# Full-height products and one transpose for the delta net's last chunk

## The chip, the cores and the metric

The kernel runs on one core of a Trainium2 chip. The metric is device time in microseconds for one execution of the whole program; lower is better. The core has a matrix engine (TensorE, PE in the profile; PEld is its weight load), a vector engine (DVE), a scalar engine (ACT), GpSimd (POOL), and DMA queues that SyncE (SP) issues here.

## The reference, cut to what matters

One inference step of a two-layer decoder trunk over 304 tokens: 16 meta tokens, 256 prompt tokens, and 8 sequences of 4 new tokens. Every layer projects the normalised input once, runs four groups of mixers beside each other (gated delta net, RG-LRU, GLA, retention), gates their outputs and projects back. The change lies in the gated delta net, in its chunked form:

```python
a = jnp.where(strict, jnp.einsum('bihk,bjhk->bhij', kb, kc) * decay, 0.0)
sol = lax.linalg.triangular_solve(a + eye, rhs, left_side=True, lower=True)
u, w = sol[..., :dv], sol[..., dv:]
v_new = u - jnp.einsum('bhik,bhkv->bhiv', w, s)
attn = jnp.einsum('bihk,bjhk->bhij', qc, kc) * decay
o = (jnp.einsum('bihk,bhi,bhkv->bihv', qc, jnp.exp(gcum), s)
     + jnp.einsum('bhij,bhjv->bihv', attn, v_new))
s_new = (s * jnp.exp(g_last)[..., None, None]
         + jnp.einsum('bjhk,bhj,bhjv->bhkv', kc, jnp.exp(g_last[..., None] - gcum), v_new))
```

There are 4 delta heads a layer, with keys and values of width 128, and each sequence has a state of 128x128.

## The kernel before

**Layout.** Activations stand transposed: 128 features on the partitions, the 304 tokens along a row. The tokens make three chunks (`CH`): 0 to 127, 128 to 255, and a last one of 48, which holds the last 16 prompt tokens and the 32 new ones (`TP` = 272 is where the new ones begin). A product contracts over partitions, so work on the last chunk contracts over 48 tokens, or over the 16 prompt tokens alone.

**Main products.** A layer's input projection is 48 tiles of 128 columns, its output projection 16. A weight tile comes in four units of 4x128 rows; ACT splits a unit into `hi`, DVE into `lo`, and PE makes three products for each 128 rows (`main<-xh,hi`, `main<-xl,hi`, `main<-xh,lo`). That is 48 main matmuls a tile. On SP the weight loads (`raw`) share one queue with all small transfers.

**Everything else** runs as threads between the main matmuls. After each main product `Threads.poll` lets every thread whose inputs are ready advance by one step; whether they are ready is reckoned by `Clocks` from prices that `price` holds for each instruction. This program runs when the kernel is built, and the order it comes to is fixed: a changed price or a changed instruction can move any later step. `take` and `give` lend buffers by the same clocks. `deltas` runs `delta_thread` for heads 0 and 1, then for heads 2 and 3; it writes PSUM tiles named d. The other mixers write tiles named e. `gate_thread` takes the outputs `o` in the order of `GATES`, heads 2 and 3 last, and makes `m`, on which the output projection waits. ACT changes its function table (an ACT_TABLE_LOAD of line 359) when a step wants Silu after Exp or Ln, or the other way.

**The end of a delta pair, line by line.** `KN[h]` holds normalised keys, padded with zeros from column 304 to 383 (line 917). `VB[h]` holds scaled values by token; its last chunk is 48 rows. `uf[h][:, 2]` is the inverse of the last chunk's triangle; its columns 64 to 127 are a copy of the new tokens' columns. Lines 1109 to 1117 scale its 48 rows into `SL` and multiply them by a constant `st` (a 48-row product for each head). Lines 1122 and 1123 transpose the last chunk's keys: 64 columns of `KN`, and then `twice` makes two matmuls with the identity that put the 32 new tokens' keys on partitions 64 to 95 and 96 to 127. `hi_lo` reads these for the state update, and line 1126 has ACT copy the 16 prompt rows into `LQ`. Lines 1137 and 1138 make the new values `VN` of the chunk, the first of the two products over 48 rows; line 1145 updates the prompt state over 16 rows; line 1153 adds the chunk's attention over 48 rows to the output. Then `o_norm` normalises the output and `stash` hands it to the gates.

Of the kernel before, what the change touches and what calls it, by code (L numbers as in the profile page):

```python
# [12 lines left out]
AF = mybir.ActivationFunctionType  # L13
# [5 lines left out]
T = 304  # L19
TP = 272  # L20
# [323 lines left out]
def trunk(ctx: ExitStack, tc: tile.TileContext, I, O):  # L344
    nc = tc.nc
    clk = Clocks()
    pe, act, dve, pool, sp = (Engine(e, k, clk) for e, k in ((nc.tensor, "P"), (nc.scalar, "A"), (nc.vector, "V"),
                                                             (nc.gpsimd, "G"), (nc.sync, "S")))
# [7 lines left out]
    def tables(func):  # L356
        want = SETS.get(func)
        if want and table[0] not in want:
            nc.scalar.preload_act_table_set(want[0])  # L359
            clk.t["A"] += 1.3  # L360
            table[0] = want[0]

    def activ(out, in_, func, **kw):
        tables(func)
        act.activation(out, in_, func, **kw)
# [35 lines left out]
    def C(name, a=0, n=1):  # L401
        return cst[:, CC[name] + a:CC[name] + a + n]
# [5 lines left out]
    ident = C("id", 0, 128)  # L408
# [8 lines left out]
    col = one.tile([128, 4, 3, 4], F32, name="col")  # L417
# [89 lines left out]
    def give(*bs):  # L507
        for b in bs:
            q = spare if b.tensor.name in lent else wides if b.shape[1] == 384 else narrows
            q.append([clk.free(b), b])  # L510
# [29 lines left out]
    def pt(tag):  # L540
        return spin(pb.tile([128, 512], F32, tag=tag, name=tag), tag, 3)
# [277 lines left out]
            pe.matmul(ps[g:g + 32, 0:128], x[:, 32 + 32 * b:64 + 32 * b], S9[:, 1 + b, :], start=b < 3, stop=b > 4)  # L819
        return ps[:, 0:128]  # L820

    def twice(out, x):

        for g in (64, 96):
            pe.matmul(out[g:g + 32], x[:, TP:T], ident, start=True, stop=True)

    def hi_lo(out, x, lo, scale=None):

        r = slice(lo, lo + 32)
# [20 lines left out]
    def advance(tag, S9, p0, n, products):  # L850
        ps = pt(tag)
        for i, (out, k, v) in enumerate(products):
            pe.matmul(ps[out, :128 * n], k, v, start=i == 0 or out.start > 0,
                      stop=i + 1 == len(products) or products[i + 1][0].start > 0)
        dve.tensor_add(S9[:, p0:p0 + n, :], S9[:, p0:p0 + n, :],
                       ps[:, :128 * n].rearrange("p (b v) -> p b v", v=128))
# [34 lines left out]
    def delta_thread(l, p, tag):  # L891
        hs = (2 * p, 2 * p + 1)
# [3 lines left out]
        K, Q, V, KN, VB, KTL, Eb, AT, qe, egl = ({} for _ in range(10))  # L896
# [11 lines left out]
        KN = dict(enumerate((yield from take(2, True))))  # L908
# [4 lines left out]
        for h in range(2):  # L913
            ps = yield from totals(tag, s[h][:, :T])
            activ(s[h][:, :T], ps[:, :T], AF.Ln, bias=eps[:, 0:1])
            activ(s[h][:, :T], s[h][:, :T], AF.Exp, scale=-0.5)
            pool.memset(KN[h][:, T:384], 0.0)
            yield
        yield from settled(*GB, *BB)
        for h in range(2):  # L920
            dve.tensor_mul(KN[h][:, :T], K[h][:, :T], s[h][:, :T])
            give(K[h], s[h])
            qe[h] = yield from take()
            activ(qe[h][:, :T], GB[h][:, :T], AF.Exp)
            activ(BB[h][:, :T], BB[h][:, :T], AF.Exp)
            pool.tensor_add(GB[h][:, :T], GB[h][:, :T], C("mask", 0, T))
            yield
        for h in range(2):
            for src, d, k in ((V, VB, 1), (KN, KTL, 3)):
                d[h] = yield from take(1, src is V)  # L930
                ps = pt(tag)
                cs = list(enumerate(CH))[:3 if src is V else 2]
                for c, (c0, n) in cs:
                    pe.transpose(ps[:n, 128 * c:128 * c + 128], src[h][:, c0:c0 + n], ident)
                for c, (c0, n) in cs:
                    activ(d[h][:n, 128 * c:128 * c + 128], ps[:n, 128 * c:128 * c + 128], AF.Copy,
                          scale=col[:n, k, c, hs[h]:hs[h] + 1])
                if src is V:
                    give(V[h])
                yield  # L940
            egl[h] = one.tile([128, 11], F32, tag=f"egl{p}{h}", name="egl")
            pool.tensor_copy(out=egl[h][:, 0:2], in_=qe[h][:, 127:256:128])
            pool.tensor_copy(out=egl[h][:, 2:11], in_=qe[h][:, 271:304:4])
            pool.tensor_mul(qe[h][:, :T], qe[h][:, :T], Q[h][:, :T])
            e = yield from take()
            for c, (c0, n) in enumerate(CH):
                activ(e[:, c0:c0 + n], GB[h][:, c0:c0 + n], AF.Exp, bias=col[:, 0, c, hs[h]:hs[h] + 1])
            give(GB[h])
            yield
            pool.tensor_mul(BB[h][:, :T], BB[h][:, :T], e[:, :T])  # L950
            pool.memset(BB[h][:, T:320], 0.0)
            AT[h] = e
            yield
        BM = BB
        for h in range(2):
# [9 lines left out]
            for a in range(4):  # L965
                src = BM[h][32 * a:32 * a + 32, :]
# [27 lines left out]
        src = dx[0:20]  # L994
# [9 lines left out]
        for h in range(2):  # L1004
            src = dx[10 * h:10 * h + 10]
# [11 lines left out]
        uf = {h: UF[h].rearrange("p (c i) -> p c i", c=3) for h in range(2)}  # L1017
        yield from settled(XB)
        dve.transpose(out=XB[:, 192:384], in_=XB[:, 0:192])
        for h in range(2):  # L1020
            for a in range(4):
                nch = 3 if a < 2 else 2
                pool.tensor_copy(out=uf[h][32 * a:32 * a + 32, 0:nch, 32 * a:32 * a + 32],
                                 in_=xb[32 * a:32 * a + 32, h, 0:nch, :])
            pool.tensor_copy(out=uf[h][0:48, 2, 64:128].rearrange("p (u s) -> p u s", u=2),
                             in_=uf[h][0:48, 2:3, 16:48].to_broadcast([48, 2, 32]))
# [41 lines left out]
        VN, SS, S9 = {}, {}, {}  # L1068
# [6 lines left out]
        ch = lambda t, c, n=128: t[:n, 128 * c:128 * c + 128]  # L1075
        ps = pt(tag)
# [5 lines left out]
        ps = pt(tag)  # L1082
# [5 lines left out]
        ps = pt(tag)  # L1088
# [6 lines left out]
        ps = pt(tag)  # L1095
# [5 lines left out]
        ps = pt(tag)  # L1101
# [5 lines left out]
        LQ, SL, R = {}, {}, {}  # L1107
        yield from settled(*S9.values())
        for h in range(2):
            SL[h] = yield from take()  # L1110
            activ(SL[h][0:48, 128:256], uf[h][0:48, 2, :], AF.Copy, scale=col[0:48, 2, 2, hs[h]:hs[h] + 1])
        yield
        ps = pt(tag)
        for h in range(2):
            pe.matmul(ch(ps, h), C("st", 0, 128)[0:48], SL[h][0:48, 128:256], start=True, stop=True)
        for h in range(2):
            activ(SL[h][:, 128:256], ch(ps, h), AF.Copy)
        for h in range(2):
            R[h], LQ[h] = yield from take(2)
            R[h] = recast(R[h], F32R)  # L1120
            pk = pt(tag)
            pe.transpose(pk[0:64, 0:128], KN[h][:, 256:320], ident)
            twice(pk[:, 0:128], KN[h])
            sc = col[:, 3, 2, hs[h]:hs[h] + 1]
            hi_lo(R[h][:, 0:128], pk[:, 0:128], 64, sc)
            activ(LQ[h][0:16, 0:128], pk[0:16, 0:128], AF.Copy, scale=sc[0:16])
            spots(lx["d"], 0, slice(0, 128), KN[h])
            spots(lx["d"], 1, slice(0, 128), qe[h])
            give(KN[h])
            yield  # L1130
            pr = reads(tag, lx["d"], S9[h])
            activ(SL[h][:, 0:128], pr, AF.Copy)
            pool.tensor_mul(S9[h], S9[h], egl[h][:, 2:11, None].to_broadcast([128, 9, 128]))
            yield
        for h in range(2):
            ps = pt(tag)
            pe.matmul(ps[:, :128], uf[h][0:48, 2, :], ch(VB[h], 2, 48), start=True, stop=False)
            pe.matmul(ps[:, :128], SL[h][:, 128:256], SL[h][:, 0:128], start=False, stop=True)
            activ(ch(VN[h], 2, 48), ps[:48, :128], AF.Copy)
            hi_lo(R[h][:, 128:256], ps[:, :128], 96)  # L1140
            give(UF[h], VB[h])
            yield
        for h in range(2):
            lq, sel = LQ[h], SL[h]
            advance(tag, S9[h], 0, 1, [(slice(0, 128), lq[0:16, 0:128], ch(VN[h], 2, 16))])
            give(KTL[h])
            yield
            ps = pt(tag)
            pe.matmul(ps[:, 0:128], ch(VN[h], 0), AT[h][:, 0:128], start=True, stop=True)
            pe.matmul(ps[:, 128:256], SS[h][:, 0:128], qe[h][:, 128:256], start=True, stop=False)  # L1150
            pe.matmul(ps[:, 128:256], ch(VN[h], 1), AT[h][:, 128:256], start=False, stop=True)
            pe.matmul(ps[:, 256:304], sel[:, 0:128], C("so", 48, 48), start=True, stop=False)
            pe.matmul(ps[:, 256:304], ch(VN[h], 2, 48), AT[h][0:48, 256:304], start=False, stop=True)
            activ(sel[:, :T], ps[:, :T], AF.Copy)
            activ(lq[:, :T], ps[:, :T], AF.Square, scale=math.sqrt(1e6 / 16384.0))
            give(SS[h], AT[h], qe[h], VN[h])
            yield
            pool.tensor_add(lq[:, :T], lq[:, :T], Q[h][:, :T])
            give(Q[h])
            yield  # L1160
            yield from o_norm(tag, l, hs[h], sel, lq, PA("na", l), 1e-6, eps[:, 1:2], eps[:, 2:3])
            give(lq)
# [589 lines left out]
    for n in (1, 1, 2, 4, 4, 4):  # L1752
        g = xf[:, k:k + n, :]
# [94 lines left out]
```

## Time and profile before

| what | value |
|---|---|
| time, median of 3 runs | 1128.61 us (1127.08 to 1130.58) |
| time of the profiled execution | 1128.37 us |
| its span, first to last instruction | 1126.4 us |
| PE busy | 1075.5 us, 95% of the span |
| DVE, ACT, POOL busy | 66%, 57%, 41% |
| mean granted TensorE clock | 0.983 |

The span leaves 2.0 us of the execution outside it. A busy PE includes pipelined matmuls that overlap, so for what a step costs PE one reads from the start of one instruction to the start of the next, not the duration printed in a row. In a row such as `48*128 48x128` the first pair is the height and width of the weights in the array, the second the moving operand. An fp32 matmul is two passes, two rows; a transpose is one.

### The profile page before, as it was taken

How to read it: one execution, taken by the hardware profiler on the slowest of the kernel's cores; microseconds unless marked ns; L12 is line 12 of the kernel's file. 1: busy time of each engine (PE TensorE's matmuls, PEld its weight loads, DVE VectorE, ACT ScalarE, POOL GpSimd, SP SyncE). 2: the span in 40 equal slices, each digit the busy share in tenths (PEclk: the TensorE clock that was granted, in tenths of full speed). 3: DMA queues.
4: the chain of work that ended last, by engine and by line, in shares of the span. 5: the costliest groups of instructions: out<-in, count | busy, mean ns of one | idle time of the engine just before them, and what ended most of it. 6: DMA issues, size and time to landing. Idle time of an engine off the chain costs nothing.

```text
span 1126.4 us, 22838 instructions
## 1 busy us (share of the span) xinstructions
PE 1075.5 (95%) x7974; PEld 1008.6 (90%) x7974; DVE 746.9 (66%) x1449; ACT 638.2 (57%) x1432; POOL 462.4 (41%) x947
## 2 busy tenths in 40 slices
PE   8999989998999999899999998999899999999996
PEld 7998979887999899899999998889789989899995
DVE  6866578678567555566568755787975575666564
ACT  6677934554754475444455875546466457645442
POOL 5423387424426833212122348554444583321110
PEclk8999989999999999899999999999999999999998
DMA  6554535455457454566544554335464755565663
GB/s 212 182 161 160 156 97 160 149 188 152 140 182 222 130 185 141 168 208 196 185 148 150 173 159 159 114 114 169 152 187 131 240 155 187 152 203 178 192 191 141
DMA packets 117058, 187.78 MB, mean 167 GB/s; under 512 B 22176, under 2 KB 45456, under 8 KB 116944
## 3 DMA queue, kind: packets, MB, share of 16 engines
q1 hardware_dynamic: 116944, 186.34, 53.5%
q8 instruction: 62, 1.02, 0.4%
q14 instruction: 52, 0.43, 0.1%
HBM read 165.09 MB, written 19.95 MB: 164 GB/s over the span
## 4 chain that ended last, share of the span: by engine, by line
PE 66%; POOL 11%; DVE 9%; DMA 5%; issue 4%; ACT 3%; SPq 1%; DVEq 0%; POOLq 0%; ACTq 0%
PE main L298 52%; PE e L298 7%; PE d L298 7%; DVE lo L298 3%; POOL s9.4_168 L298 3%; DMA raw<-in_w_in_dram 2%; POOL s9.3_11274 L298 2%; POOL n L298 2%; DVE n L298 2%; POOL m L298 1%; POOL s9.0_6106 L298 1%; DVE m L298 1%; DVE zq L298 1%; SPq L298 1%; DVE acc L298 1%
## 5 line engine op out<-in xcount | busy, mean ns | idle before, releaser
L298 PE MATMUL main<-xh,hi 128*128 128x304 f32 (+2 forms) x1488 | 471.8, 317 | 2.2 <-ACT xh L298 2.2
L298 PE MATMUL main<-xh,lo 128*128 128x304 f32 (+2 forms) x1488 | 453.0, 304 | 11.5 <-DVE lo L298 11.3
L298 DVE TENSOR_TENSOR lo<-raw,hi 128x512 fp32r<-128x512 f32 (+1 forms) x513 | 389.0, 776 | 111.8 <-ACT hi L298 104.0
L298 ACT ACTIVATE hi<-raw 128x512 fp32r<-128x512 f32 (+1 forms) x513 | 317.5, 626 | 251.5 <-PE main L298 113.1
L298 PE MATMUL main<-xl,hi 128*128 128x304 f32 (+2 forms) x1488 | 450.5, 303 | 0.3 <-DVE xl L298 0.2
L298 PEld LDWEIGHTS main<-xh,hi 128*128 128x128 f32 x1488 | 284.0, 191 | 16.4 <-issue 8.7
L298 PEld LDWEIGHTS main<-xh,lo 128*128 128x128 f32 x1488 | 283.9, 191 | 16.5 <-DVE lo L298 16.4
L298 PEld LDWEIGHTS main<-xl,hi 128*128 128x128 f32 x1488 | 284.6, 191 | 2.8 <-DVE xl L298 1.1
L298 PE MATMUL main<-m,hi 128*128 128x304 f32 (+1 forms) x1024 | 211.3, 301 | 0.0
L298 PEld LDWEIGHTS main<-m,hi 128*128 128x128 f32 x1024 | 168.1, 190 | 3.7 <-issue 2.9
L298 PE MATMUL main<-m,lo 128*128 128x304 f32 (+1 forms) x512 | 154.4, 302 | 2.0 <-DVE lo L298 2.0
L298 POOL TENSOR_TENSOR ssq<-ssq,n 128x304 f32<-128x304 f32 (+1 forms) x29 | 34.9, 1203 | 175.6 <-ACT n L298 175.6
L298 PEld LDWEIGHTS main<-m,lo 128*128 128x128 f32 x512 | 96.9, 189 | 2.2 <-DVE lo L298 2.2
L298 POOL COPY cvo<-ct 128x3 f32<-128x3 f32 x64 | 32.4, 534 | 116.1 <-DVE ct L298 116.0
L298 POOL TENSOR_TENSOR n<-n,n 128x304 f32<-128x304 f32 (+1 forms) x38 | 35.1, 937 | 91.6 <-ACT n L298 65.4
L298 ACT ACTIVATE n<-n 128x304 f32<-128x304 f32 (+4 forms) x114 | 47.8, 439 | 42.6 <-DVE n L298 34.4
L298 DVE TENSOR_TENSOR n<-main,n 128x304 f32<-128x304 f32 (+1 forms) x32 | 14.9, 466 | 62.7 <-PE main L298 47.6
L298 DVE SCALAR_TENSOR_TENSOR acc<-ct,par,acc 128x328 f32<-128x328 f32 x64 | 42.7, 667 | 6.1 <-ACT acc L298 4.8
L298 ACT ACTIVATE m<-m 128x304 f32<-128x304 f32 (+6 forms) x101 | 42.1, 433 | 5.4 <-PE d L298 3.2
L359 ACT ACT_TABLE_LOAD x33 | 42.3, 1283 | 0.6
L298 ACT ACTIVATE n<-e 128x304 f32<-128x304 f32 (+5 forms) x65 | 19.3, 307 | 28.0 <-PE e L298 13.8
L298 DVE TENSOR_TENSOR n<-main,rstd 128x304 f32<-128x304 f32 (+1 forms) x40 | 18.6, 464 | 24.8 <-PE main L298 24.7
(410 smaller groups left out, 1410.5 us busy)
## 6 DMA issues: line engine op xcount, KB each, us to landing
raw<-in_w_in_dram SPq DMA_DIRECT2D x383, 256.0 KB
raw<-in_w_out_dram SPq DMA_DIRECT2D x128, 256.0 KB
n<-o_dram SPq DMA_DIRECT2D x27, 152.0 KB
m<-in_x_dram SPq DMA_DIRECT2D x16, 152.0 KB
o_dram<-m SPq DMA_DIRECT2D x16, 152.0 KB
n<-in_x_dram SPq DMA_DIRECT2D x16, 152.0 KB
xs_dram<-n SPq DMA_DIRECT2D x16, 152.0 KB
n<-xs_dram SPq DMA_DIRECT2D x16, 152.0 KB
```

What stands on the lines that cost most here:

```text
L298: r = f(*a, **k)
L359: nc.scalar.preload_act_table_set(want[0])
```

## The change

It has four parts. The products of lines 1111 to 1115, 1137, 1145 and 1153 take all 128 rows of their operands. For that `VB`'s last chunk and `LQ` are cleared to zero first by POOL, and ACT writes all 128 rows of `VN`'s last chunk and of `SL`. In `KN` the columns 320 to 383 are no longer zeros but two copies of the 32 new tokens' keys, made by POOL after the keys are normalised; the attention built from them is masked to zero on those rows. One transpose of `KN`'s last 128 columns then gives the 16 prompt rows and the two copies at once, and `twice` is gone. No line of the scheduler is changed.

```diff
-    def twice(out, x):
-        for g in (64, 96):
-            pe.matmul(out[g:g + 32], x[:, TP:T], ident, start=True, stop=True)
...
-            pool.memset(KN[h][:, T:384], 0.0)
+            pool.memset(KN[h][:, T:320], 0.0)
...
             dve.tensor_mul(KN[h][:, :T], K[h][:, :T], s[h][:, :T])
+            pool.tensor_copy(out=KN[h][:, 320:384].rearrange("p (u t) -> p u t", u=2),
+                             in_=KN[h][:, None, TP:T].to_broadcast([128, 2, 32]))
...
+                if src is V:
+                    pool.memset(d[h][:, 256:384], 0.0)
...
-            activ(SL[h][0:48, 128:256], uf[h][0:48, 2, :], AF.Copy, scale=col[0:48, 2, 2, hs[h]:hs[h] + 1])
+            activ(SL[h][:, 128:256], uf[h][:, 2, :], AF.Copy, scale=col[:, 2, 2, hs[h]:hs[h] + 1])
...
-            pe.matmul(ch(ps, h), C("st", 0, 128)[0:48], SL[h][0:48, 128:256], start=True, stop=True)
+            pe.matmul(ch(ps, h), C("st", 0, 128), SL[h][:, 128:256], start=True, stop=True)
...
-            pe.transpose(pk[0:64, 0:128], KN[h][:, 256:320], ident)
-            twice(pk[:, 0:128], KN[h])
+            pe.transpose(pk[:, 0:128], KN[h][:, 256:384], ident)
+            pool.memset(LQ[h][:, 0:128], 0.0)
...
-            pe.matmul(ps[:, :128], uf[h][0:48, 2, :], ch(VB[h], 2, 48), start=True, stop=False)
+            pe.matmul(ps[:, :128], uf[h][:, 2, :], ch(VB[h], 2), start=True, stop=False)
...
-            activ(ch(VN[h], 2, 48), ps[:48, :128], AF.Copy)
+            activ(ch(VN[h], 2), ps[:, :128], AF.Copy)
...
-            advance(tag, S9[h], 0, 1, [(slice(0, 128), lq[0:16, 0:128], ch(VN[h], 2, 16))])
+            advance(tag, S9[h], 0, 1, [(slice(0, 128), lq[:, 0:128], ch(VN[h], 2))])
...
-            pe.matmul(ps[:, 256:304], ch(VN[h], 2, 48), AT[h][0:48, 256:304], start=False, stop=True)
+            pe.matmul(ps[:, 256:304], ch(VN[h], 2), AT[h][:, 256:304], start=False, stop=True)
```

The built orders of layer 0 are the same but for these instructions, the added POOL ones and a few DVE rows that change places with a neighbour. From the first delta pair of layer 1 on, steps of the threads stand at other places among the main matmuls.

On PE, layer 1, second delta pair: the two `st` products (from n_161 and n_11275) and the key transposes of the pair's first head (g_135 is `KN`), before:

```order
L298 MATMUL main<-xh,lo 128x288
L298 MATMUL d<-n_161,cst 128x128
L298 MATMUL d<-n_11275,cst 128x128
L298 MATMUL d<-cst,g_135 64x128
L298 MATMUL d<-cst,g_135 32x128 x2
L298 MATMUL main<-xh,hi 128x288
```

The same place after:

```order
L298 MATMUL main<-xh,lo 128x288
L298 MATMUL d<-n_157,cst 128x128
L298 MATMUL d<-n_146,cst 128x128
L298 MATMUL d<-cst,g_135 128x128
L298 MATMUL main<-xh,hi 128x288
```

One instruction stands where three did; this group has moved from behind main matmul 5088 to behind 5160 of the program's 6144, and layer 1's input projection ends with 5376.

On ACT, layer 1, where the second delta pair's q, k and v go through Silu (n_6105, n_147 and n_151 here) while GLA's last level is in Exp (n_10036), before:

```order
L298 ACTIVATE n_10036<-n_10036 128x304
L298 ACTIVATE hi<-raw 128x512
L359 ACT_TABLE_LOAD
L298 ACTIVATE n_6105<-n_6105 128x304
L298 ACTIVATE n_147<-n_147 128x304
L298 ACTIVATE n_151<-n_151 128x304
L298 ACTIVATE hi<-raw 128x512 x2
```

After (Silu on n_156, n_5629, n_151 and on n_153, n_147, n_10076; Exp on n_149):

```order
L359 ACT_TABLE_LOAD
L298 ACTIVATE n_156<-n_156 128x304
L298 ACTIVATE n_5629<-n_5629 128x304
L298 ACTIVATE n_151<-n_151 128x304
L359 ACT_TABLE_LOAD
L298 ACTIVATE n_149<-n_149 128x304
L298 ACTIVATE hi<-raw 128x512
L359 ACT_TABLE_LOAD
L298 ACTIVATE n_153<-n_153 128x304
L298 ACTIVATE n_147<-n_147 128x304
L298 ACTIVATE n_10076<-n_10076 128x304
```

An Exp now stands between the two heads' Silus, with a table load on each side of it.

On ACT, the end of layer 1: the last head's normalisation (the rows with eps) and the Silus of the last gates, before:

```order
L298 ACTIVATE n_12492<-d,eps 128x304
L298 ACTIVATE n_12492<-n_12492,eps 128x304
L298 ACTIVATE hi<-raw 128x512 x2
L359 ACT_TABLE_LOAD
L298 ACTIVATE n_152<-n_152 128x288
L298 ACTIVATE n_10368<-n_10368 128x288
L298 ACTIVATE hi<-raw 128x512 x2
L298 ACTIVATE m_12837<-n_152 128x288
L298 ACTIVATE m_12839<-n_10368 128x288
L298 ACTIVATE hi<-raw 128x512 x6
L298 ACTIVATE n_12493<-n_12493 128x288
L298 ACTIVATE n_6105<-n_6105 128x288
```

After:

```order
L359 ACT_TABLE_LOAD
L298 ACTIVATE n_12656<-d,eps 128x304
L298 ACTIVATE n_12656<-n_12656,eps 128x304
L298 ACTIVATE hi<-raw 128x512 x5
L359 ACT_TABLE_LOAD
L298 ACTIVATE n_3615<-n_3615 128x288
L298 ACTIVATE n_151<-n_151 128x288
```

The last gates' Silus now have a table load right ahead of them; the gates before the last have moved ahead of the last head's normalisation. Over the whole program ACT has 38 table loads after and 34 before.

## Rows read from the trace of the kernel before

**Rows 1.** The page's chain that ended last: shares of the span by engine.

```profile
PE 66%; POOL 11%; DVE 9%; DMA 5%; issue 4%; ACT 3%; SPq 1%; DVEq 0%; POOLq 0%; ACTq 0%
```

**Rows 2.** Stretches 215-251, 421-450, 745-781, 958-990 us: their length and busy times, summed.

```profile
sum 133.00, PE 132.49 PEld 117.85 DVE 91.12 ACT 72.50 POOL 55.04; mean PE 33.12 PEld 29.46 DVE 22.78 ACT 18.12 POOL 13.76
```

**Rows 3.** Stretches, PE alone: length, busy (instructions), granted clock, DMA share, GB/s.

```profile
60.00:464.00 404.00, 386.51 (x2884) 0.98 0.52 158
600.00:1018.00 418.00, 399.77 (x3061) 0.99 0.52 161
```

**Rows 4.** Timeline of PE, a head's output: start us, duration us, instruction.

```profile
987.81 0.38 PE L298 MATMUL d<-n,g 128*128 128x128 f32 x2
988.03 0.39 PE L298 MATMUL d<-n,n 128*128 128x128 f32 x2
...
988.48 0.32 PE L298 MATMUL d<-cst,n 128*128 128x48 f32 x2
988.73 0.42 PE L298 MATMUL d<-n,g 48*128 48x48 f32 x2
...
989.31 0.29 PE L298 MATMUL main<-xl,hi 128*128 128x288 f32 x1
```

**Rows 5.** Timeline of PE, two full-height 48-column products ahead of main ones.

```profile
867.38 0.32 PE L298 MATMUL d<-g 128*128 128x48 f32 x2
867.53 0.39 PE L298 MATMUL d<-n,g 128*128 128x48 f32 x2
...
867.97 0.30 PE L298 MATMUL main<-xl,hi 128*128 128x304 f32 x1
```

**Rows 6.** Timeline of PE, the `st` products and three transposes of layer 1.

```profile
958.87 0.29 PE L298 MATMUL main<-xh,lo 128*128 128x288 f32 x1
959.09 0.71 PE L298 MATMUL d<-n,cst 48*128 48x128 f32 x4
959.73 0.64 PE L298 MATMUL d<-cst,g 128*64 128x128 f32 x5
...
960.54 0.29 PE L298 MATMUL main<-xl,hi 128*128 128x288 f32 x1
960.67 0.29 PE L298 MATMUL main<-xh,lo 128*128 128x288 f32 x1
```

**Rows 7.** Timeline of PE, two full transposes ahead of main matmuls.

```profile
106.31 0.38 PE L298 MATMUL d<-cst,g 128*128 128x128 f32 x2
...
106.67 0.30 PE L298 MATMUL main<-xl,hi 128*128 128x304 f32 x1
```

**Rows 8.** Timeline of PE, the prompt state's 16-row product.

```profile
975.28 0.29 PE L298 MATMUL main<-xh,lo 128*128 128x288 f32 x1
975.51 0.48 PE L298 MATMUL d<-g,n 16*128 16x128 f32 x2
...
976.16 0.29 PE L298 MATMUL main<-xl,hi 128*128 128x288 f32 x1
```

**Rows 9.** Groups by shape: count, busy us, mean ns, idle us before them.

```profile
L298 PE MATMUL d<-g,g 48*128 48x128 f32 x16 | 3.9, 323 | 0.0
L298 PE MATMUL d<-g,n 16*128 16x128 f32 x16 | 3.9, 322 | 0.0
```

**Rows 10.** Groups by shape, POOL.

```profile
L298 POOL COPY m<-m 128x64 f32<-128x64 f32 x14 | 3.9, 312 | 6.1 <-PE e L298 6.1
L298 POOL MEMSET g<- 128x128 f32 x16 | 2.8, 203 | 0.0
```

**Rows 11.** Timeline of ACT, the copy of 16 rows into `LQ` (idle before it, releaser).

```profile
967.03 0.36 ACT L298 ACTIVATE n<-d,col 16x128 f32<-16x128 f32 x1 [1.60 <-POOL lxd L298]
```

**Rows 12.** Groups, ACT: the table loads.

```profile
L359 ACT ACT_TABLE_LOAD x33 | 42.3, 1283 | 0.6
```

**Rows 13.** Timeline of DVE, the last head's output is normalised.

```profile
995.11 0.53 DVE L298 SCALAR_TENSOR_TENSOR n<-n,par,n 128x304 f32<-128x304 f32 x1 [1.03 <-ACT n L298]
```

**Rows 14.** Timeline of PE, first output tile of layer 1.

```profile
1017.50 0.40 PE L298 MATMUL main<-m,lo 128*128 128x288 f32 x1 [2.01 <-DVE lo L298]
```

## The prediction

> **What bounds the kernel now.** I read the chain that ended last first: two thirds of it is PE, a tenth each POOL and DVE [rows 1]. So time taken from PE is worth having where PE leads, and I looked next at the four stretches that hold the changed instructions (two delta pairs in each of two layers). They come to 133.00 us, and PE is busy for 132.49 of them [rows 2]: there nothing else ends a wait. Over a layer's input projection PE stands idle for 404.00 - 386.51 = 17.5 us in layer 0 and for 18.2 us in layer 1 [rows 3]. The two layers do the same work in two different interleavings, and the idle sums agree within a microsecond; that is my measure of what another interleaving does.
>
> **What a tile shape costs.** Prices are from start to start. A full-height product of 128 columns takes 988.03 - 987.81 = 0.22 us, a main matmul 0.13 (960.54 to 960.67) [rows 4, 6]. The array's shape in use shows in the rows: wherever a 48-row, 16-row or narrow-output instruction follows or precedes a full one, the next start comes about 0.1 us late. So a short product is dearer than a full one, and so are its neighbours.
>
> **The change, part by part.**
>
> *The `st` products* (a pair of heads at once). From the main matmul at 958.87 to the transposes at 959.73 are 0.86 us [rows 6]. At full height this is 0.13 + 2 x 0.22 = 0.57. Saved: 0.29 a pair, 4 pairs: 1.2 us.
>
> *The transposes.* From 959.73 to the second main matmul after them, 960.54, are 0.81 us for three instructions and one main matmul [rows 6]. Two full transposes and a main matmul took 0.36 (106.31 to 106.67) [rows 7], so 0.36 - 0.13 = 0.23 for two and 0.11 for one; with a main matmul 0.24. Saved: 0.57 a head, 8 heads: 4.6 us.
>
> *The 16-row product of the prompt state.* From 975.28 to 976.16 are 0.88 us [rows 8], at full height 0.13 + 0.22 + 0.13 = 0.48. Saved 0.40, 8 times: 3.2 us.
>
> *The 48-row product of the new values.* Its passes stand in the same number and at the same mean as the 16-row ones, 16 at 323 ns against 16 at 322 [rows 9], and it too stands between full-height neighbours: 0.40, 8 times, 3.2 us.
>
> *The 48-row product into the output.* It moves only 48 columns, and a full-height product of that kind costs hardly less than one of 128 columns. From a full 48-column product at 988.48 to the second main matmul at 989.31 are 0.83 us [rows 4]; the same with both products full, 867.38 to 867.97, are 0.59 [rows 5]. Saved 0.24, 8 times: 1.9 us.
>
> Sum on PE: 1.2 + 4.6 + 3.2 + 3.2 + 1.9 = **14.1 us**. All of it lies where PE has no idle time [rows 2]. Further on PE waits now and then for steps that a thread began behind an earlier PE instruction; those begin earlier too, so the saving isn't handed back at the next wait.
>
> *ACT's wider writes* (128 partitions for 48) have the same 128 columns: no cost taken.
>
> *POOL.* Eight copies of 64 columns at 0.312 and sixteen clears of 128 columns at 0.203 [rows 10] are 2.5 + 3.2 = 5.7 us more in all, with the old clears a little shorter. The copy waits for DVE's keys; behind it on POOL stands the addition of the mask to the gates, which waits for ACT's Exps in any case. The matmuls that read the copies come steps later. The clear of `LQ` is a new thing that ACT waits for, with its next weight split behind it; but this ACT copy waited 1.60 us for POOL already [rows 11]. Bounds: 0 with POOL idle over half the span, 5.7 if every POOL microsecond were on the chain; at POOL's 11% of the chain 0.6. A few DVE and POOL waits shorten with the earlier PE as well, so I take 0.
>
> *The order.* The scheduler isn't edited, but its clocks read the new instructions, and layer 1 comes out differently. The last delta pair starts its end 72 main matmuls later on PE, and ACT gets four more table loads, at 1283 ns each [rows 12]: 5.1 us of ACT. Two more lie around GLA's last Exps, two in the last pair. Bounds on the end: below nothing (another interleaving can also wait less), and 5.1. The one right ahead of the last gates' Silus has no cover that I can name, since the output projection waits on those gates; the others have three weight units split ahead. I take one load: **1.3 us**.
>
> *The late last pair.* From the `st` products at 959.09 to the end of the last head's normalisation at 995.11 + 0.53 = 995.64 [rows 6, 13] are 36.6 us. After the change 5376 - 5160 = 216 main matmuls follow those products before the projection ends, 28 us, and the first output tile has three of its four weight units ahead of the last gates, 12 times three main matmuls, 5 us more. Main matmuls alone thus cover 33 of the 36.6, and the other threads' PE work among them, which I have not counted, covers the rest. Before, the wait in the first output tile ended at 1017.50 [rows 14], 22 us after that head was ready: it was not what ended the wait, but the last gate tiles were, which the projection makes at its very end. So I let the 72 matmuls cost nothing; the bound is 3.6.
>
> Against the profiled execution, 1128.37 us (the runs' median is 1128.61): 1128.4 - 14.1 + 1.3 = **1115.6 us**.
>
> **A rule that speaks against it.** In rows, the short products already run as tiles of the array: 48*128, 16*128, 128*64. The Trainium skill, TensorEngine Tiling (Array Packing), section When to Use Tiling, wants just that: row tiling where the contraction is 64 or less, column tiling where the output is. By it the full-height form is the wrong direction. The same page (Key Properties) says that a change of tiling mode drains the engine; the trace agrees with that, at about 0.1 us for each side of a short product.
>
> **Rivals.**
> 1. *The saving is given back in layer 1.* The new order brings waits of its own: the gates and GLA's levels queue behind the extra table loads and the moved POOL steps. Price: layer 1's half of the saving, 7 us, and up to the other 3.8 us of table loads: 1128.4 - 7 = 1121.4, up to 1125. For it: 38 loads instead of 34, and threads up to 87 main matmuls later. Against: the two interleavings seen differ by 0.7 us of idle time [rows 3].
> 2. *Tiles were as cheap as they are small.* The late starts around short products would then be something else, such as the wait for the operand, and go on after the change. Left would be the two instructions fewer in each head's transposes, which on the same rows is at most 4.6 us: 1128.4 - 4.6 + 1.3 = 1125.1. This is what the rule of the page above comes to here. Against: the late start is the same 0.2 us in every such group, with operands long ready.
> 3. *The last pair becomes the end of layer 1: slower.* Its chain of 36.6 us then outlasts what covers it. 33 us are covered for certain (above); beyond that it costs microsecond for microsecond. The kernel is slower by over 0.3% (1131.8) when the chain takes over 33 + 14.1 - 1.3 + 3.4 = 49 us, and at 52 us it gives 1128.4 - 12.8 + 19 = 1134.6. For it: table loads within the chain and all weight splits in the same queues. Against: it would need 12 us more than the 36.6 measured, with the PE work in it shorter than before.
> 4. *The change doesn't do what it says*, the instruction count staying as it was: excluded, since the built order has the single transposes.
>
> **How the numbers follow.** Forecast, 0.70: 1115.6, with a range of its own of 1109 to 1121; its lower end is a new order that saves as much as one third of layer 1's 18.2 us of waits, its upper end four loads on the path. Given back in layer 1, 0.19: 1121 to 1125, with a tail to within 0.3%. Tiles, 0.05: 1125. Last pair, 0.06: up to 1135, of which 0.04 beyond 1131.8. A measurement of this kernel tells apart about 0.3%, 3.4 us. Faster means under 1125.0: 0.70 + 0.16 + 0.03 = 0.89; slower, over 1131.8: 0.04; the rest, 0.07, is within. The range for 8 times in 10 takes the forecast's and most of the first rival: 1109 to 1123.
>
> **What would show it.** Each step on its rows after the change: a 128x128 transpose with the next main matmul at 0.24 us; products `128*128` in place of `48*128` and `16*128`, 0.22 apart; no late main matmul behind them. PE's busy time falls by some 14 us, and the end of layer 0's input projection, whose order is unchanged, comes 7 us earlier: that tests the prices without the new order. PE's idle time in layer 1 stays near 18 us; if it is 25, rival 1 holds. In the first output tile a wait near 2 us; if it is 10, ended by the last head's output, rival 3 has begun. The prediction is wrong if a full-height product with zeros takes longer than the full ones now, or if PE's saved time returns as waits already in layer 0.

## The result

| | median | runs |
|---|---|---|
| before | 1129.59 us | 4, 1127.08 to 1131.96 |
| after | 1117.94 us | 4, 1115.10 to 1119.42 |

The changed kernel takes 0.9895 of the time, 95% interval 0.9872 to 0.9919: 11.9 us less (9.1 to 14.4, on 1128.4). The forecast was 1115.6. The profiled execution after took 1119.42 us, with a span of 1117.5 (before 1128.37 and 1126.4).

First the page of after, busy times and the chain that ended last, as in [rows 1]:

```profile
PE 1064.9 (95%) x7942; PEld 1005.9 (90%) x7942; DVE 736.9 (66%) x1449; ACT 643.6 (58%) x1436; POOL 462.2 (41%) x971
...
PE 68%; POOL 13%; DVE 7%; DMA 5%; issue 3%; ACT 3%; SPq 1%; DVEq 0%; POOLq 0%; ACTq 0%
```

PE still leads. Then PE by stretches. They are cut at the same main matmuls in every kernel from here on: from number 600 (behind the start, which by then differs by 1.4 us; the first changed instruction, a clear on POOL, itself starts 1.5 us later than before, so the change didn't make that) to the end of layer 0's input projection, through layer 0's output projection, and from there to the 24th main matmul of layer 1's first output tile. Columns as in [rows 3]. First before, which stands ahead only in other cuts, then after:

```profile
110.66:455.62 344.96, 332.78 (x2536) 0.99 0.52 157
455.62:576.75 121.13, 117.14 (x802) 0.97 0.60 192
576.75:1013.45 436.70, 420.47 (x3202) 0.99 0.52 161
```

```profile
112.03:450.42 338.39, 325.52 (x2519) 0.99 0.53 160
450.42:571.92 121.50, 117.52 (x802) 0.97 0.61 192
571.92:1004.12 432.20, 415.65 (x3187) 0.98 0.53 162
```

Layer 0's projection is 6.6 us shorter, layer 1's stretch 4.5. PE's idle time in layer 1 is 436.70 - 420.47 = 16.2 before and 432.20 - 415.65 = 16.6 after, so what layer 1 lacks isn't idle time; the granted clock is lower. Each of these lengths is from a single profiled execution. Executions of one kernel differ (the kernel before took 1125.7 to 1136.1 us over all its runs, with a standard deviation of some 2.4), so a difference of 2 us in a length may be the execution's.

The timeline of PE after, at the places of [rows 6], [rows 8] and [rows 4]:

```profile
959.78 0.30 PE L298 MATMUL main<-xh,lo 128*128 128x288 f32 x1
959.92 0.60 PE L298 MATMUL d<-n,cst 128*128 128x128 f32 x4
960.36 0.27 PE L298 MATMUL d<-cst,g 128*128 128x128 f32 x1
...
960.61 0.29 PE L298 MATMUL main<-xl,hi 128*128 128x288 f32 x1
...
972.85 0.30 PE L298 MATMUL main<-xh,lo 128*128 128x288 f32 x1
972.98 0.38 PE L298 MATMUL d<-g,n 128*128 128x128 f32 x2
973.12 0.38 PE L298 MATMUL main<-xh,hi 128*128 128x288 f32 x1
973.34 0.29 PE L298 MATMUL main<-xl,hi 128*128 128x288 f32 x1
```

The `st` products, the transpose and the next main matmul take 960.61 - 959.78 = 0.83 us, where before 1.67 passed. The 16-row product, now at full height, takes 973.34 - 972.85 = 0.49 with its neighbours, forecast 0.48.

One place where layer 1 loses is its end. From the timeline of all engines there, after; then the same head's `lq` in the kernel before; then PE's granted clock over two stretches, after:

```profile
985.85 2.35 POOL L298 TENSOR_TENSOR s9.3_13077<-n,cst 128x1024 fp32r<-128x1024 f32 x1
...
986.37 4.22 DVE L298 TENSOR_TENSOR m<-n,m 128x288 fp32r<-128x288 f32 x2
...
988.16 2.11 POOL L298 TENSOR_TENSOR s9.2_13113<-n,cst 128x1024 fp32r<-128x1024 f32 x1
988.25 0.30 PE L298 MATMUL d<-hq,onesr 128*128 128x304 f32 x1
990.51 0.68 DVE L298 TENSOR_TENSOR lo<-raw,hi 128x512 fp32r<-128x512 f32 x1
991.11 0.46 DVE L298 TENSOR_TENSOR lq<-n,hq 128x304 fp32r<-128x304 f32 x1
...
991.62 0.62 PE L298 MATMUL d<-lq,onesr 128*128 128x304 f32 x1 [3.08 <-DVE lq L298]
```

```profile
991.37 2.11 DVE L298 TENSOR_TENSOR lq<-n,hq 128x304 fp32r<-128x304 f32 x1
```

```profile
789.84:793.25 3.41, 3.41 (x16) 0.50 0.42 109
991.22:994.64 3.42, 3.02 (x12) 0.50 0.29 77
```

POOL builds the two spread values of the last pair back to back (a spread value is a head's 128 columns times a mask, once for each of the 8 sequences: 1024 elements). Two DVE products that started meanwhile take 4.22 us, until POOL is done, where without POOL beside them they take 0.82 (experiment 4); a `lo` and then `lq` come behind them, and PE waits 3.08 us for `lq`. In the kernel before POOL's two products start 10 us apart; `lq` is held beside the first, and PE waits 0.87 us. Then PE runs 3.42 us at half the clock (1.2 GHz). Over layer 1's stretch, PE has 13.7 us at that level after and 6.8 before: the 6.9 more cost at most half of that, 3.4 us (2.7 by the part of them in which PE was busy). The clock's part differs between executions: in the two runs of experiment 7, which keep this order, PE waits 2.91 us at this place, and no stretch at half the clock follows.

### The profile page after: what moved, and what is told of

Read it like the earlier page. It is cut to its first block, busy times and chain, and to the rows that moved or that the text cites. A ratio compares the mean times of both kernels' runs of the same rounds, so it can differ in the third digit from the quotient of the medians.

```text
span 1117.5 us, 22819 instructions
## 1 busy us (share of the span) xinstructions
PE 1064.9 (95%) x7942; PEld 1005.9 (90%) x7942; DVE 736.9 (66%) x1449; ACT 643.6 (58%) x1436; POOL 462.2 (41%) x971
## 4 chain that ended last, share of the span: by engine, by line
PE 68%; POOL 13%; DVE 7%; DMA 5%; issue 3%; ACT 3%; SPq 1%; DVEq 0%; POOLq 0%; ACTq 0%
PE main L298 54%; PE e L298 7%; PE d L298 7%; POOL s9.4_168 L298 4%; DMA raw<-in_w_in_dram 3%; POOL s9.0_6110 L298 2%; DVE lo L298 2%; POOL s9.3_11360 L298 2%; POOL n L298 2%; POOL m L298 2%; DVE n L298 1%; DVE m L298 1%; ACT L359 1%; SPq L298 1%; ACT hi L298 1%
```

## The experiments

Ratios are to the kernel before, run beside each experiment on the same chip, where its median was 1131.0 to 1131.1 us. The profile of the kernel before is of an execution of 1128.37 us, 2.7 below that, so against it a stretch of another kernel looks up to that much longer than it would against a typical execution. The first two hold the order of one kernel and issue the instructions of the other. A `ghost` charges the planner's clocks without issuing; `.real` issues without charging.

**1. The new instructions in the old order.**

```diff
+    def ghost(kind, name, out, ins=(), cols=0):
+        clk.op(kind, price(kind, name, size(out), out, cols), [out], list(ins))
...
-            pool.memset(KN[h][:, T:320], 0.0)
+            pool.real.memset(KN[h][:, T:320], 0.0)
+            ghost("G", "memset", KN[h][:, T:384])
...
             pe.transpose(pk[:, 0:128], KN[h][:, 256:384], ident)
-            pool.memset(LQ[h][:, 0:128], 0.0)
+            for g in (64, 96):
+                ghost("P", "matmul", pk[g:g + 32, 0:128], [KN[h][:, TP:T], ident], None)
+            pool.real.memset(LQ[h][:, 0:128], 0.0)
...
```

> The changed kernel's instructions in the order of the kernel before: the planner is charged for the old clears and the three transposes, so that on every engine the rows stand as before, but for the new ones (33 table loads, as before). Theory A (the PE prices of the prediction hold, 14.1 us, and about 4 of them are given back in the changed kernel by its new order at the end of layer 1): 14 us below the kernel before, 12.5 to 15.5, that is a ratio near 0.9875, no wait of 3 us on PE at the end of layer 1's input projection that the kernel before doesn't have, main matmul 5400 about 14 us earlier than before. Rival B (the saving comes back as waits whatever the order, since what PE waits for there runs on other engines): 10 to 11.5 us below, as the changed kernel.

Measured: 1127.79 us, 0.9973 (0.9957 to 0.9989), 3 us less and not 14. Theory A is wrong on the sum, and B too. PE by stretches:

```profile
112.08:450.76 338.68, 325.27 (x2519) 0.99 0.55 160
450.76:571.35 120.59, 116.61 (x801) 0.99 0.63 193
571.35:1014.00 442.65, 421.27 (x3186) 0.98 0.54 159
```

Layer 0 gains 6.3 us, as in the changed kernel; layer 1 becomes 6 us longer than in the profile of before. Since the order is the same, each edited group can be set against itself, start to start, up to the second main matmul behind it. Where no wait falls into one, the `st` products with the first transpose save 0.85 us, the second transpose 0.54, the 48-row product of the new values 0.39, the 16-row product 0.39, the product into the output 0.26, in both layers. So PE does save 4 x 0.85 + 4 x 0.54 + 8 x (0.39 + 0.39 + 0.26) = 13.9 us, and layer 1, in these two profiles, gives back its half and 6 us more. The longest wait in it:

```profile
898.26 4.18 DVE L298 TENSOR_TENSOR n<-n,s9.0_6110 128x304 f32<-128x304 f32 x2
898.49 0.83 POOL L298 TENSOR_TENSOR n<-n,s9.0_6110 128x304 f32<-128x304 f32 x1
899.28 0.83 POOL L298 TENSOR_TENSOR g<-g,s9.0_6110 128x304 f32<-128x304 f32 x1
900.08 1.54 POOL L298 TENSOR_TENSOR n<-n,n 128x288 f32<-128x288 f32 x2
...
902.74 1.51 DVE L298 TENSOR_TENSOR lo<-raw,hi 128x512 fp32r<-128x512 f32 x2
...
903.58 0.40 PE L298 MATMUL main<-xh,lo 128*128 128x288 f32 x1 [3.17 <-DVE lo L298]
```

It is the same kind of event: two DVE products of 304 elements, which took 1.08 us before, are held for 4.18 beside four POOL products, and the weight's low part (`lo`) comes late. It isn't wholly new. In the kernel before the same four POOL products hold another DVE product, and PE waits 2.10 us for `lo` 24 main matmuls further on:

```profile
900.71 2.62 DVE L298 TENSOR_TENSOR n<-n,n 128x304 f32<-128x304 f32 x1 [1.01 <-POOL n L298]
```

Three waits of 1.53, 1.28 and 1.53 us stand where before has none over 0.25. Idle time in the stretch is 442.65 - 421.27 = 21.4 us, 5.1 more than before, and PE has 20.5 us at half the clock, 13.7 more, worth at most 6.8. For these two profiles that accounts for all but 1 us: 436.7 - 6.9 + 5.1 + 6.8 = 441.7, measured 442.65. Over all executions the clock's part is smaller: the mean granted clock of the whole program is 0.9824 here (12 runs) and 0.9849 before (29), an estimate of 0.0025 x 1128 = 2.8 us.

**2. The old instructions in the new order** (the reverse: the copies and clears are ghosts, `twice` is issued uncharged).

> The instructions of the kernel before in the order of the changed kernel: the planner is charged for the changed kernel's copies and clears and for one transpose, and emits the old ones; 37 table loads in the profile instead of 33. Theory A (the order by itself costs about 4 us, at the end of layer 1): 3 to 5 us slower than the kernel before, with PE waiting near 3 us for DVE's rows while POOL makes its two products of 1024 elements back to back. The prediction's own term: 1.3 us slower. Rival B (the order costs nothing): within 0.5 us.

Measured: 1128.00 us, 0.9975 (0.9955 to 0.9995). The wait is there, behind POOL's two products:

```profile
1003.26 0.41 PE L298 MATMUL d<-lq,onesr 128*128 128x304 f32 x1 [2.70 <-DVE lq L298]
```

But the order as a whole isn't slower, as theory A and the prediction's term had it; it is 2.8 us faster (0.6 to 5.1), with 37 table loads against 33. So this wait belongs to the order. Where the 2.8 us come from isn't shown: layer 1's stretch is 438.24 us in this profile, 1.5 longer than before, and its idle time 16.7 against 16.2. With the new order held, the instructions alone are worth about 9 us (5.5 to 12.5, from both intervals): from 0.9975 here to 0.9895.

**3. Parts of the change, in the old order.** Only the transposes (with the copies); only the products (with the clears); only POOL's additions. The edits are those of experiment 1, each without the others.

> Only the transposes changed, in the order of the kernel before; the products stay at 48 and 16 rows. By the prediction's step, 0.57 us a head: 4.6 us below the kernel before, and in the trace the transpose of 128x128 with the next main matmul at 0.24 us. If the late starts around the short products had nothing to do with the shape of the tile, the saving would be at most that of two instructions without their late neighbours, 8 x 2 x 0.13 = 2.1 us.

> Only the products at full height (with the sixteen clears), three transposes as before, in the order of the kernel before. By the prediction's prices 9.5 us of PE, 4.75 in each layer. Theory A (PE's prices hold and the loss in layer 1 comes from PE arriving earlier at steps that other engines set, with the clock at half after the new waits): layer 0's input projection 4 to 5 us earlier, and of layer 1's 4.75 nothing or less left, 2 to 5 us below before in all. Rival B (the loss comes with the copies on POOL, which this kernel does not have): 9 us below before.

> The kernel before with the changed kernel's POOL instructions alone (eight copies, sixteen clears more, the old clears shorter); PE's products and its three transposes stay, and the order on every engine is that of the kernel before but for the new rows. Theory A (POOL's additions cost nothing, as the prediction took): within 1.5 us of the kernel before. Rival B (they move POOL's steps by a microsecond or two, into DVE's way, and that is what the transposes alone lost 8 us by in layer 1): 3 to 8 us slower than before, with layer 0's input projection as before and the loss in layer 1.

| lengths, us | layer 0's projection | layer 1's stretch | time, ratio |
|---|---|---|---|
| before | 344.96 | 436.70 | 1 |
| transposes | 342.67 | 442.73 | 1.0028 (1.0011 to 1.0045) |
| products | 341.02 | 442.52 | 0.9976 (0.9958 to 0.9994) |
| POOL's additions | 345.55 | 439.90 | 1.0025 (1.0010 to 1.0041) |
| all, old order | 338.68 | 442.65 | 0.9973 (0.9957 to 0.9989) |
| old instructions, new order | 344.41 | 438.24 | 0.9975 (0.9955 to 0.9995) |
| after | 338.39 | 432.20 | 0.9895 (0.9872 to 0.9919) |

Layer 0 adds up: 2.3 + 3.9 = 6.2, and POOL's additions cost nothing that counts there. Layer 1 doesn't: in these profiles each part in the old order makes it 3 to 6 us longer, POOL's additions too, which touch nothing on PE. The lengths overstate it, for the reason given above, and for the products most: their profiled execution, 1131.87 us, was 3.5 above their median. By the ratios, which take in every run, of the forecast 4.6 us of the transposes and 9.5 of the products 7.8 and 6.8 are lost. For the transposes, both forecasts failed (3.2 us slower); POOL's 2.8 us (1.1 to 4.6) are nearer to rival B's 3 to 8 than to A's 1.5, but shut out neither; for the products theory A held, with 3.9 us in layer 0 for its 4 to 5. One place of the POOL run shows what a step moved by a microsecond meets:

```profile
859.02 1.28 POOL L298 TENSOR_TENSOR s9.3_11176<-m,cst 128x512 fp32r<-128x512 f32 x1
859.32 0.28 DVE L298 TENSOR_TENSOR s9.0_6118<-s9.0_6118,e 128x128 f32<-128x128 f32 x1
859.51 2.57 DVE L298 TENSOR_TENSOR lo<-raw,hi 128x512 fp32r<-128x512 f32 x2
```

The two `lo`, which took 0.68 and 1.00 us in the kernel before, are held; the addition at 859.32, which takes one operand from PSUM (`e`), isn't. PE then waits 1.28 us for the `lq` behind them, where before it didn't wait.

**4. The last pair's spreads later, in layer 1.** First behind the last gates; then also with PE's products on them 16 polls later (the last two added lines, in the second run alone).

```diff
         for h in range(2):
+            while l and p and not all(("m", l, k) in got for k in range(KT)):
+                yield
             vm = recast((yield from take9()), F32R)
             spread(vm[:, 0:8], R[h], C("m8", 0, 8))
             yield
+            for _ in range(16 if l and p else 0):
+                yield
```

> The changed kernel, with one step moved: the last delta pair of layer 1 begins POOL's two products of 1024 elements only when the last gates are ready; all else stands as in the changed kernel up to there. Theory A (DVE operations that start while such a product runs are stretched until it ends; that held back the row that PE waited 3.08 us for, and the clock fell after it): two DVE products of 128x288 that took 4.22 us for both take about 0.9, the PE wait there falls under 1 us, the clock stays up, and the time is 3 to 4.5 us below the changed kernel, some 15 us below the kernel before. Rival C (what PE waits for there is late anyway, by its ACT steps): the same time as the changed kernel, 10 to 11.5 us below before.

> The changed kernel with the last pair's two POOL products of 1024 elements begun when the last gates are ready, as in the run with the spreads later, and PE's products on them put 16 polls later still, so that PE need not wait 4.72 us for POOL there. Theory A (DVE held by POOL, then the clock, took 4 to 6 us at this place, and the last run only moved the wait to PE's products): both waits gone, 4 to 6 us below the changed kernel, 15 to 17 below before, ratio near 0.986. Rival C (something else at the end of layer 1 is late anyway, such as the last gates): 0 to 2 below the changed kernel.

Measured: 1118.09 us, 0.9885 (0.9859 to 0.9911), and 1118.58, 0.9891 (0.9867 to 0.9915): neither faster than the changed kernel. In the first, the two DVE products took 0.82 us and PE's wait of 3.08 was gone; but PE then waited for the spread itself:

```profile
982.88 0.82 DVE L298 TENSOR_TENSOR m<-n,m 128x288 fp32r<-128x288 f32 x2
...
998.03 1.22 PE L298 MATMUL d<-s9.3_13134,n 128*128 128x512 f32 x2 [4.43 <-POOL s9.3_13134 L298]
```

In the second, one of the last gates' DVE products and the `lo` behind it were held beside POOL:

```profile
998.44 2.11 POOL L298 TENSOR_TENSOR s9.3_13134<-n,cst 128x1024 fp32r<-128x1024 f32 x1
...
998.99 1.88 DVE L298 TENSOR_TENSOR m<-n,m 128x288 fp32r<-128x288 f32 x1 [0.20 <-ACT m L298]
...
1003.22 0.50 PE L298 MATMUL main<-m,lo 128*128 128x288 f32 x1 [3.59 <-DVE lo L298]
```

Theory A had the mechanism right and the price wrong, rival C the reverse: here a collision that was moved was paid at its new place.

**5. The spreads on DVE**, in the changed kernel and its order.

```diff
-        pool.tensor_mul(vm, R[:, None, 128:256].bitcast(F32).to_broadcast([128, n, 128]),
-                        blocks[:, :, None].to_broadcast([128, n, 128]))
+        dve.real.tensor_mul(vm, *ins)
+        ghost("G", "tensor_mul", vm, ins)
```

> The changed kernel with all 24 products of 1024 or 512 elements that build the spread values issued on DVE instead of POOL, in the same place of the program and with the planner charged as before, so that the order is unchanged. POOL loses some 35 us, DVE gains some 20. Theory A (while POOL makes such a product DVE stands still anyway): DVE's busy time rises by well under 20 us, the stretched DVE instructions of layer 1 become fewer, and the time falls by 2 to 6 us against the changed kernel. Rival B (DVE's own work in front of the splits and rows that PE waits for costs as much as the lock): same time within 1.5 us, or slower.

Measured: 1118.63 us, 0.9894 (0.9871 to 0.9918), as the changed kernel: rival B. DVE took over work of 21.4 us (eight products at 1.22, sixteen at 0.68 but for two of 1.33) and POOL's busy time fell by 33.2, yet its own busy time rose by only 3.7, from 736.9 to 740.6. The other 17.7 were thus time in which it had been held. But PE now waits 3.52 and 2.39 us in layer 0's projection for spread values that DVE makes, and no longer 3.98 us for POOL's behind it: the projection became 5.1 us longer (343.51), the output projection 5.7 shorter (115.76).

**6. The last pair's spreads out of everybody's way, in both layers**: 12 polls behind the gates, PE's products 10 polls behind them; in the changed kernel and in the kernel before.

```diff
+            while p and not all(("m", l, k) in got for k in range(KT)):
+                yield
+            for _ in range(12 if p else 0):
+                yield
             vm = recast((yield from take9()), F32R)
             spread(vm[:, 0:8], R[h], C("m8", 0, 8))
             yield
+            for _ in range(10 if p else 0):
+                yield
```

> The changed kernel with the last delta pair's two POOL products of 1024 elements put 12 polls behind the last gates, in both layers, and PE's products on them 10 polls later still. At the end of layer 0 PE waits 4.29 + 0.59 us for POOL there in every kernel so far, with the clock at half behind it; in layer 1 the changed kernel waits 3.08 us for DVE held by POOL, and the two runs that moved the products in layer 1 waited 4.72 for the products or 3.88 us for the last gates' rows, which DVE made late beside them. Theory A (each of these is the same collision in a new place, and none is there when the products stand behind the gates' rows): layer 0's wait gone with its clock stretch, 5 to 8 us, layer 1's down to about 2 us, 3 to 5 us: 8 to 12 us below the changed kernel, 1106 to 1110 on this chip. Rival C (another step is late there anyway): 0 to 4 us below.

> The same move of the last pair's POOL products in the kernel before. Theory A: layer 0's wait gone as in the changed kernel, 5 to 8 us; in layer 1 there is less to gain, 0 to 2. So 5 to 9 us below the kernel before; and the difference to the changed kernel with the same move comes nearer to the 14 us of PE, 12 to 15, since the end of layer 1 no longer takes 4 of them. Rival: the difference between the two stays at 11.

Measured: 1108.96 us, 0.9814 (0.9784 to 0.9844), the fastest of all and by the ratios 9 us below the changed kernel (5 to 13), and 1122.48, 0.9927 (0.9900 to 0.9954). Theory A's totals came out in both, 8 to 12 us and 5 to 9, if not quite where they lie: in the first, layer 0 gave 2.4 us for its 5 to 8. Between the two lie 13.5 us by their medians and 12.8 by their means, 9.1 to 16.5; that doesn't tell theory A's 12 to 15 from the rival's 11. The first run by stretches, its waits in the first output tiles, and, from the changed kernel, the wait at the end of layer 0 that is gone:

```profile
111.33:449.88 338.55, 326.10 (x2518) 0.98 0.54 160
449.88:568.78 118.90, 117.09 (x804) 0.99 0.64 196
568.78:993.70 424.92, 413.49 (x3183) 0.99 0.55 164
```

```profile
457.14 0.41 PE L298 MATMUL main<-m,lo 128*128 128x304 f32 x1 [1.81 <-DVE lo L298]
...
997.63 0.40 PE L298 MATMUL main<-m,lo 128*128 128x288 f32 x1 [1.89 <-DVE lo L298]
```

```profile
456.24 1.22 PE L298 MATMUL d<-s9.0_6080,n 128*128 128x512 f32 x2 [3.98 <-POOL s9.0_6080 L298]
```

Against the changed kernel, layer 0's output projection is 2.6 us shorter and layer 1's stretch 7.3; some 2 of these are the last pair's products on PE, which now stand behind the end of the stretch (what follows it is 2.0 us longer). In the kernel before with the same move they take 117.36 and 433.88 us, and layer 0's input projection 343.29: the two kernels differ by 4.7 us there and by 9.0 in layer 1's stretch, not by 7 in each, so a sum near PE's price is in part chance.

**7. One more product a head in the output group**, short (the first line, one run) or full (the second, another), in the changed kernel; the product behind it overwrites its result.

```diff
+            pe.real.matmul(ps[:, 256:304], ch(VN[h], 2, 48), AT[h][0:48, 256:304], start=True, stop=True)
+            pe.real.matmul(ps[:, 256:304], ch(VN[h], 2), AT[h][:, 256:304], start=True, stop=True)
```

> The changed kernel with one more product a head, of 48 rows by 48 columns, set between full-height products of the output group (its result is overwritten by the next product there). Theory A (a short product between full ones pays for two changes of the array's shape): the group grows by about 0.4 us a head. Rival 2 of the prediction (tiles as cheap as they are small): by 0.1 us at most.

> The same with all 128 rows: the group grows by about 0.15 to 0.22 us a head, less than by the short one, though it multiplies more.

Measured, in all eight groups: 0.54 us more with the short one (0.54 to 0.55), 0.22 with the full one (0.22 to 0.23). The timelines of PE, short, then full:

```profile
982.46 0.39 PE L298 MATMUL d<-n,g 128*128 128x128 f32 x2
982.77 0.42 PE L1151 MATMUL d<-n,g 48*128 48x48 f32 x2
983.12 0.42 PE L298 MATMUL d<-cst,n 128*128 128x48 f32 x2
983.38 0.39 PE L298 MATMUL d<-n,g 128*128 128x48 f32 x2
```

```profile
983.84 0.39 PE L298 MATMUL d<-n,g 128*128 128x128 f32 x2
984.06 0.32 PE L1151 MATMUL d<-n,g 128*128 128x48 f32 x2
984.22 0.39 PE L298 MATMUL d<-cst,n 128*128 128x48 f32 x2
984.44 0.39 PE L298 MATMUL d<-n,g 128*128 128x48 f32 x2
```

The short one starts 0.31 us behind its neighbour and the next one 0.35 behind it; the full one 0.22 and 0.16. The one that multiplies more is cheaper by 0.3 us: theory A, at 0.54 us for its 0.4, and not rival 2.

## Why the prediction was right, point by point

*PE's prices*: right, each within 0.03 us. Forecast per group 0.29 / 2 + 0.57 for a head's `st` and transpose on average, 0.40, 0.40, 0.24; measured 0.70 (0.85 and 0.54 for the two heads), 0.39, 0.39, 0.26; in all 13.9 against 14.1. Rival 2 fell: experiment 7 measures the lone short product. The Trainium skill's rule on where to use tiles (TensorEngine Tiling (Array Packing), When to Use Tiling) speaks for the short form, and here the measurement decides against it: these short products stand alone among full ones, and one of them costs 0.54 us where the full one costs 0.22.

*Layer 0 as the test of the prices*: forecast 7 us, measured 6.6. Its order isn't quite unchanged, though: seven groups of PE's matmuls stand 3 or 6 main matmuls later. In the old order the measure is 6.3. *PE's busy time*: forecast -14, measured -10.6. That was a poor measure: busy durations overlap, and they grow at half the clock.

*POOL's additions, taken as 0*: mis-sized. They cost 2.8 us by themselves in the old order (1.1 to 4.6), within the bounds given. The step that failed was to ask only who waits for the copies and clears. They also move POOL's other steps, and one place shows such a step in DVE's way; that all of the 2.8 us come so isn't shown.

*The order, taken as 1.3 us by a table load*: wrong in size and sign, -2.8 us (-5.1 to -0.6). If the added loads cost anything, the order gained more elsewhere.

*The sum*: that it came within 1 us of the measured 11.9 is in part luck. These two errors nearly cancel, and the terms didn't add either: the new instructions are worth 3 us in the old order and 9 in the new one, of 14 on PE. The step that failed there is the sentence that the saving isn't handed back at the next wait, because steps begin earlier too. A DVE step held by POOL doesn't begin earlier. In the changed kernel layer 1 keeps 4.5 us of 7: that is rival 1 at a third of its price, and as clock, not as the idle time by which the prediction meant to see it (16.6 us, near the 18 that spoke against the rival). Whether the change is worth its full price with the collisions at the ends of both layers out of the way isn't settled: 12.8 us there, 9.1 to 16.5, against 11.9 without.

*The measure for another interleaving* (two idle sums within 0.7 us) was too kind: layer 1's stretch spreads over 424.9 to 442.7 us in these kernels, for PE work that differs by 7 (and by some 2 more where the last pair's products stand behind it).

*The late last pair, taken as 0*: right; PE's wait in layer 1's first output tile was 0.47 us, for `lo`, and rival 3 didn't begin.

**Open.** Which of the old order's new waits costs how much wasn't tried one by one. That DVE held by POOL, and the clock after a wait, make up the loss in layer 1 is argued, not shown: it rests on the rows and the sum in experiment 1 and on experiment 6, which took two of these collisions away and gained about as much in the kernel before (8.3 us) as in the changed one (9). Experiment 5 took POOL's largest products away and gained nothing, and in experiment 4 the waits came back elsewhere. Why the new order keeps more of PE's saving than the old one is open too.

## What to carry to other kernels

Price a PE edit by starts, neighbours included, and test the price in a stretch whose order is unchanged: here it was right to a few hundredths of a microsecond. Then look for what else is set by time and not by order, here which DVE instruction starts while POOL runs a long one, since a saving, or added clears of 0.2 us, that shift these can lose more than they gain. Before judging a change small, clear the places where every version waits: moving two POOL products in each layer took another 9 us off the changed kernel, and 8 off the kernel before.

## What the runs showed of the hardware

- DVE products with both inputs in SBUF were held beside POOL's products. Two of 288 elements took 4.22 us instead of 0.82 while POOL built its spread values, and moving POOL's products to DVE, 21.4 us of work there, raised DVE's busy time by 3.7. An addition with one operand in PSUM wasn't held (0.28 us). The Trainium skill (SBUF — State Buffer, Who interferes with whom) says that a DVE instruction with two inputs in SBUF contends with a GpSimd one that reads SBUF, and that the ports they share are an exclusive lock. The rows agree. They also show a DVE product, in experiment 1, held for 3.69 us, over four POOL products that started after it.
- A single product of 48 rows among full ones cost 0.54 us, the same at full height 0.22.
- A long wait of PE is mostly followed by a stretch at half the granted clock. Of 58 waits of 2.5 us or more in the 14 profiles, from 60 to 1095 us of each, 52 had one begin during them or within 4 us of their end, and 6 had none. Such a stretch lasted 3.4 or 6.8 us, which cost up to 1.7 or 3.4; the same wait of 4.0 us at the end of layer 0 was followed by either, in runs of the same order.
